# Splitting weight chunks three ahead of the one in use, in place of two

## The chip, the cores and the metric

The kernel runs on one core of a Trainium2 chip. The time is that of the device for one execution, in microseconds (us); lower is better. Names used below: TensorE (PE; its weight loads are listed as PEld), VectorE (DVE), ScalarE (ACT), GpSimd (POOL) and SyncE (SP, whose queue issues most loads).

## What is computed

Two consecutive layers of an encoder over 256 positions of 2048 channels, all in float32.

```python
h = rms_norm(x, norm_mix[layer])
if layer % 2 == 0:   # one input projection: pooling channels, queries, keys, values
    mixed = concatenate([pool_out, att_out]) @ w_out_ab[e]     # multi-scale pooling, 12-head attention (4 key heads)
else:
    mixed = mlstm_mixer(h, w_in_c[o], b_gate_c[o], h_norm_c[o], w_out_c[o])   # 8 heads, both directions
x = x + mixed
x = x + conv_ffn(rms_norm(x, norm_ffn[layer]), w_up[layer], conv_w[layer], conv_b[layer], w_down[layer])
```

`conv_ffn` is an up-projection to 2 x 5632 channels, a width-3 convolution over positions, a SiLU gate and a down-projection back to 2048.

## The kernel before

**Weights in chunks.** All the weights pass once through the core as a single list of 881 chunks, each 128 partitions by 1024 float32 (512 KB). TensorE multiplies in the float32r format, so each operand is cut in two: a high part, which is a cast, and a low part, which is the rest. A product is then high times high, high times low and low times high. For a chunk of weights this is `split` (L123): a cast on ScalarE (L134; on VectorE for the very first piece) and a subtraction on VectorE (L135), into a tile `hl` that holds both parts.

**Buffers.** Raw chunks go into the pool `wraw` (L230), which has 6 buffers; split chunks into `wsplit` (L231), which has 4. So the load of chunk k must wait for the split of k-6, and the split of chunk k for TensorE's last matmul with k-4.

**How far ahead.** The class `Stream` (L93) keeps the list. TensorE's code calls `next` (L154) for each chunk, and that calls `ahead`, which first issues what lies ahead and then hands out the chunk. `la` is how many chunks ahead loads are issued (5), `sa` how many ahead splits are issued. `st = Stream(nc, behind, wp, sp, weights, 5, 2)` at L247 sets both; in `attention_layer` `sa` is 1 during the key projection and is set again at L733.

```python
def ahead(self, i, split=None):                       # L142
    n = len(self.srcs)
    ...
    while self.n_load < min(n, i + self.la + 1):
        if self.n_load >= self.n_split + self.la - self.sa + 1:
            self.split()
        self.load()
    while self.n_split < min(n, i + (self.sa if split is None else split) + 1):
        self.split()
```

Some chunks of the down-projection are sums of two or more pieces of weights. They go through a tile `sum` (3 buffers): a load on SP (L119) and a DMA on GpSimd's queue that adds (L120), and for the chunk that follows, two adds on VectorE (L130, L131).

**Order of the work.** TensorE's order is that of the code. ScalarE, VectorE, SP and GpSimd are ordered when the program is built, by a scheduler that works from a model of the times and takes the order of the code as the priority (the key projection alone is fixed by hand on ScalarE, VectorE and SP too). Each engine then runs its list strictly in order. So the place in the code at which a split is issued sets its priority against the rest of ScalarE's and VectorE's work.

**The stages.** First the key projection (`kproj`), the first query projection (`qproj0`), values, further queries with the attention heads woven in between, the two pooling groups, and the output projection (`op`). Then the FFN of layer 0: 44 up-projections (`up`, 64 matmuls of 4 chunks each; `stat_group`, L374), and between them units of a down-projection with fewer products (Winograd's form of Strassen's scheme, `pp`, `unit` at L1035). Their products are drained from PSUM by `drain` (L1069, adds at L1081) and put together by `total` (L1091, L1098). Each up-projection is followed by a gather (L438, L439), a multiplication (L996), six convolution steps on ScalarE (L1001 to L1003), two adds on VectorE (L1004, L1005), the gate (L1009, L1010) and a split of the result (L1011, L1012); `combine` (L1014) makes the sums of operands (L1018 to L1025). The last slice of channels goes through an ordinary down-projection in four blocks of 512 columns (`dn`, `down_two` at L1148, `down` at L1132). Its tiles come from the pool `mm` of two PSUM tiles, and `residual` (L445, L448) adds each block to `x` in two halves; when both halves have been read, the tile is free for the block after next. Where a layer follows, `norm.add` squares the new block on ScalarE (L345) and transposes it on TensorE (L323). Then the second mixer (`mv`, `mq`, `mk`, `mo`, `op`) and the FFN of layer 1, which ends with the output.

Beside this run premix DMAs (L485), issued on ScalarE's and GpSimd's queues and paced by TensorE's matmuls, which add pieces of down-projection weights in DRAM ahead of their use.

Of the kernel before, what the change touches and what calls it, by code (L numbers as in the profile page):

```python
# [216 lines left out]
def trunk(ctx: ExitStack, tc: tile.TileContext, gx, xT, xn, call, catt, cml, weights, mixes, out):  # L217
# [29 lines left out]
    st = Stream(nc, behind, wp, sp, weights, 5, 2)  # L247
# [165 lines left out]
    def mov_group(act, name, width=512, before=None, after=None):  # L413

        ps = mmp.tile([P, 2, 512 if width > 256 else width], F32, tag="mm", name=name)
        per = CH * P // width
        hl = None
        for k in range(KT):
            if k % per == 0:
                before and before(k)  # L420
                hl = st.next()
                after and after(k)
            src = act(k)
            c = (k % per) * width
            terms = [(t, i, j) for t in range(2) for i, j in ((0, 0), (0, 1), (1, 0))]
            if before and k == 0:
                terms.sort(key=lambda e: e[1:])
            for t, i, j in terms:
                first, last = k == 0 and (width > 256 or t == 0), k == KT - 1 and (width > 256 or t == 1)
                mm(ps[:, t, :width], src[:, i, t * P : t * P + P], hl[:, j, c : c + width],  # L430
                   first and i + j == 0, last and i == 1)
            wv.tick(1.29 * width / 512)
        return ps
# [60 lines left out]
    def attention_layer(norm, nxt):  # L494
        with ExitStack() as es:
# [234 lines left out]
            st.split(then)  # L730
            st.sa = 1
            ps = mov_group(xx, "kproj", 512, ahead, tables)
            st.sa = 2  # L733
            first.close()
            catb.extend(actp.tile([P, 8, 2, S], F32R, tag=f"B{i}", name=f"cat{i}") for i in range(2))
            wv.add(k_block(ps))
# [452 lines left out]
    norms = [Norm(0), None]  # L1189
    norms[1] = Norm(1)  # L1190
    attention_layer(norms[0], norms[1])
    norms.append(Norm(2))
    ffn_layer(0, norms[1], norms[2])
# [265 lines left out]
```

## Time and profile before

| | us |
|---|---|
| three runs | 2162.14, 2163.13, 2166.14 |
| median | 2163.13 |
| the profiled execution's own time | 2162.39 |
| its span, from the first to the last instruction | 2160.3 |

The granted TensorE clock was 1.000 over the span. HBM was read and written at 294 GB/s over the span. Loads of 512 KB took 4.7 to 5.6 us at the median from issue to landing, and the two DMAs of a sum 5.7 and 9.6 us.

How to read the rows: a group row has line, engine, operation, tile written and tiles read, shape and count, and then busy time, mean in ns, idle time before it and what ended most of that. A row of waits has who waited for whom, the total in us, the number of times and the longest. A row of the timeline has start, length, engine, line, operation and count, and in brackets the idle time before it and what ended it. A row of the chain of waits has start, length and name: the chain is followed back from the last instruction, at each step to what released it. Ends of matmuls are modelled, so the starts are the better guide to TensorE's pace.

### The profile page before, as it was taken

How to read it: one execution, taken by the hardware profiler on the slowest of the kernel's cores; microseconds unless marked ns; L12 is line 12 of the kernel's file. 1: busy time of each engine (PE TensorE's matmuls, PEld its weight loads, DVE VectorE, ACT ScalarE, POOL GpSimd, SP SyncE). 2: the span in 40 equal slices, each digit the busy share in tenths (PEclk: the TensorE clock that was granted, in tenths of full speed). 3: DMA queues.
4: the chain of work that ended last, by engine and by line, in shares of the span. 5: the costliest groups of instructions: out<-in, count | busy, mean ns of one | idle time of the engine just before them, and what ended most of it. 6: DMA issues, size and time to landing. Idle time of an engine off the chain costs nothing.

```text
span 2160.3 us, 31974 instructions
## 1 busy us (share of the span) xinstructions
PE 2151.2 (100%) x11394; PEld 1840.4 (85%) x11394; DVE 1752.4 (81%) x2453; ACT 1421.7 (66%) x2219; POOL 225.2 (10%) x286
## 2 busy tenths in 40 slices
PE   9999999999999999999999999999999999999999
PEld 7888888888888888889888888888888888888887
DVE  7676678899889888987777676667889898988988
ACT  7665577767677767766454544457877777776774
POOL 0012111111100100001111111211100010100000
PEclk9999999999999999999999999999999999999999
DMA  9668989899989877778888887888978897987675
GB/s 327 211 202 240 294 247 312 248 314 304 297 297 290 294 258 234 265 239 249 229 253 244 242 248 227 273 272 251 289 226 290 286 290 264 280 271 253 228 252 196
DMA packets 167281, 566.24 MB, mean 262 GB/s; under 512 B 21098, under 2 KB 23698, under 8 KB 167122
## 3 DMA queue, kind: packets, MB, share of 16 engines
q1 hardware_dynamic: 130640, 467.54, 61.7%
q0 software_dynamic: 22240, 56.90, 15.7%
q10 hardware_dynamic: 14242, 39.77, 5.8%
q8 instruction: 89, 1.46, 0.3%
q14 instruction: 70, 0.57, 0.1%
HBM read 561.98 MB, written 73.44 MB: 294 GB/s over the span
## 4 chain that ended last, share of the span: by engine, by line
PE 91%; DVE 3%; DMA 3%; ACT 1%; issue 1%; ACTq 0%; DVEq 0%; POOLq 0%
PE up L272 41%; PE pp L272 14%; PE op L272 8%; PE mv L272 4%; PE mq L272 4%; PE mk L272 4%; PE mo L272 4%; PE dn L272 3%; PE qproj L272 3%; DVE hl L135 2%; DMA sum<-in_dn 1%; DMA w<-in_up 1%; PE vproj L272 1%; PE kproj L272 1%; PE av L272 1%
## 5 line engine op out<-in xcount | busy, mean ns | idle before, releaser
L135 DVE TENSOR_TENSOR hl<-w,hl 128x1024 fp32r<-128x1024 f32 (+2 forms) x843 | 1014.4, 1215 | 207.6 <-ACT hl L134 204.6
L134 ACT CAST hl<-w 128x1024 fp32r<-128x1024 f32 (+2 forms) x842 | 866.3, 1047 | 440.2 <-PE up L272 138.4
L272 PE MATMUL up<-xx,hl 128*128 128x512 f32 (+1 forms) x5632 | 994.2, 337 | 0.9 <-DVE hl L135 0.9
L272 PEld LDWEIGHTS up<-xx,hl 128*128 128x128 f32 x5632 | 866.8, 188 | 131.7 <-DVE hl L135 1.9
L272 PE MATMUL pp<-hl,s 128*128 128x512 f32 x888 | 221.8, 391 | 1.6 <-DVE hl L135 1.5
L272 PEld LDWEIGHTS pp<-hl,s 128*128 128x128 f32 x888 | 163.4, 188 | 36.3 <-DVE hl L135 4.7
L485 POOL DMA_DIRECT2D m<-m x136 | 108.4, 799 | 743.8 <-PE up L272 347.2
L272 PE MATMUL pp<-hl,g 128*128 128x512 f32 x666 | 169.5, 390 | 0.0
L272 PEld LDWEIGHTS pp<-hl,g 128*128 128x128 f32 x666 | 122.4, 188 | 23.7
L438 ACT COPY tb_up<-up 128x512 f32<-128x512 f32 x88 | 51.6, 587 | 120.6 <-PE up L272 120.6
L485 POOL DMA_DIRECT2D m<-in_dn x68 | 57.0, 838 | 601.1 <-PE up L272 271.5
L1004 DVE TENSOR_TENSOR y<-y,z 128x510 f32<-128x510 f32 x88 | 60.6, 689 | 53.5 <-ACT y L1003 53.4
L1003 ACT ACTIVATE y<-tb_up,conv 128x256 f32<-128x256 f32 x176 | 103.7, 589 | 0.0
L439 DVE TENSOR_TENSOR tb_up<-up,tb_up 128x512 f32<-128x512 f32 x88 | 60.7, 690 | 42.0 <-ACT tb_up L438 41.4
L272 PE MATMUL mk<-xx,hl 128*128 128x512 f32 (+1 forms) x512 | 92.2, 337 | 0.0
L272 PE MATMUL mq<-xx,hl 128*128 128x512 f32 (+1 forms) x512 | 92.2, 337 | 0.0
L1001 ACT ACTIVATE z<-tb_up,conv 128x256 f32<-128x256 f32 x176 | 88.4, 502 | 5.2 <-DVE tb_up L996 4.3
L272 PE MATMUL mv<-hl,xx 128*128 128x512 f32 (+2 forms) x480 | 91.7, 350 | 0.0
L272 PE MATMUL op<-hl,cat 128*128 128x512 f32 x384 | 91.5, 393 | 0.0
L272 PE MATMUL mo<-hl,xx 128*128 128x512 f32 x384 | 90.5, 391 | 0.0
L272 PE MATMUL op<-hl,mcat 128*128 128x512 f32 x384 | 89.5, 392 | 0.0
L272 PEld LDWEIGHTS mq<-xx,hl 128*128 128x128 f32 x512 | 79.3, 188 | 11.6
(233 smaller groups left out, 2171.8 us busy)
## 6 DMA issues: line engine op xcount, KB each, us to landing
w<-in_up SPq DMA_DIRECT2D x352, 512.0 KB, 5.1
w<-in_dn SPq DMA_DIRECT2D x179, 512.0 KB, 5.0
w<-in_m_in SPq DMA_DIRECT2D x124, 512.0 KB, 5.6
m<-in_dn ACTq DMA_DIRECT2D x136, 256.0 KB, 5.5
w<-m SPq DMA_DIRECT2D x68, 512.0 KB, 4.8
w<-in_a_in SPq DMA_DIRECT2D x46, 512.0 KB, 4.7
sum<-in_dn SPq DMA_DIRECT2D x40, 512.0 KB, 5.7
sum<-in_dn POOLq DMA_DIRECT2D x40, 512.0 KB, 9.6
```

Of the source, the lines that this page charges most:

```text
L134: (self.nc.vector.tensor_copy if i + c == 0 else self.nc.scalar.copy)(hl[:, 0, c : c + n], w[:, c : c + n])
L135: low = self.nc.vector.tensor_sub(hl[:, 1, c : c + n], w[:, c : c + n], hl[:, 0, c : c + n].bitcast(F32))
L272: last_mm[0] = pe.matmul(out_, lhsT, rhs, start=start, stop=stop, skip_group_check=True)
L438: a.copy(tb, ps[:, :, 1, :])
L439: v.tensor_add(tb, ps[:, :, 0, :], tb)
L485: paced(eng.dma_start(to[p : p + P // 2], src[p : p + P // 2], **kw))
L1001: a.activation(z[:, 0, j, :], u[:, j, :], AF.Copy, scale=cw(tl, 0))
L1003: a.activation(y[:, j, :], u[:, j, :], AF.Identity, scale=cw(tl, 1), bias=cw(tl, 3))
L1004: v.tensor_add(y[:, :, 1:S], y[:, :, 1:S], z[:, 0, :, 0 : S - 1])
```

## The change

```diff
             st.split(then)
             st.sa = 1
             ps = mov_group(xx, "kproj", 512, ahead, tables)
-            st.sa = 2
+            st.sa = 3
             first.close()
```

From the first query projection to the end of the kernel, the call for chunk i issues splits up to i+3 in place of i+2. Loads are still issued up to i+5, and the pools keep their 6 and 4 buffers. The number of instructions is the same.

## The prediction

> **What bounds the kernel now.** I read the page first, then the waits of TensorE (PE and PEld), of ScalarE and of the SP queue, and last the timeline at the places where TensorE stops.
>
> ```profile
> PE 2151.2 (100%) x11394; PEld 1840.4 (85%) x11394; DVE 1752.4 (81%) x2453; ACT 1421.7 (66%) x2219; POOL 225.2 (10%) x286
> ...
> PE 91%; DVE 3%; DMA 3%; ACT 1%; issue 1%; ACTq 0%; DVEq 0%; POOLq 0%
> ...
> L135 DVE TENSOR_TENSOR hl<-w,hl 128x1024 fp32r<-128x1024 f32 (+2 forms) x843 | 1014.4, 1215 | 207.6 <-ACT hl L134 204.6
> L134 ACT CAST hl<-w 128x1024 fp32r<-128x1024 f32 (+2 forms) x842 | 866.3, 1047 | 440.2 <-PE up L272 138.4
> ```
>
> TensorE is busy for 2151.2 of 2160.3 us, so whatever the splits do, at most some 9 us can be won. A split is one cast on ScalarE (1.05 us) and one subtraction on VectorE (1.22 us). The next rows say what they wait for, and what waits for them (us in total, times, longest).
>
> ```profile
> PE pp L272 <- DVE hl L135: 1.5, 3, 0.7
> PE wps L296 <- DVE pad L694: 1.2, 1, 1.2
> PE up L272 <- DVE hl L135: 0.9, 1, 0.9
> ```
>
> ```profile
> PEld pp L272 <- DVE hl L135: 4.7, 8, 1.1
> PEld up L272 <- DVE hl L135: 1.9, 3, 1.3
> ```
>
> ```profile
> ACT hl L134 <- PE up L272: 151.7, 118, 1.8
> ```
>
> ```profile
> SPq L114 <- DVE hl L135: 1332.5, 638, 7.0
> ```
>
> All that TensorE waits for late splits after the first projection is 1.5 + 0.9 = 2.4 us of idle, or 4.7 + 1.9 = 6.6 us if every wait of the weight loads is counted. Splits are seldom late. They are themselves held by TensorE: there are four buffers of split weights, so the cast of chunk k starts when TensorE has left chunk k-4, and ScalarE stands idle for that (151.7 us under the up-projection alone). The loads in turn hang on the splits that free their buffers (1332.5 us). Three ahead plus the one in use are the same four buffers. So the change cannot run a split before TensorE releases its buffer. It can only change what stands in front of it on ScalarE and VectorE.
>
> **What the change moves.** The built program of after has the same instructions as that of before, on every engine. TensorE's order is the same to the last one. About 64 of ScalarE's 2277 entries and 228 of VectorE's 2423 stand elsewhere. SP has one load (chunk 543) a few places earlier, ahead of loads of sums. GpSimd has one premix DMA ahead of one accumulating DMA. Both are moved long before their data is used, and I cost them at nothing: what hides them is the out-projection of the second mixer, and if it didn't, one load is late by one issue. Nearly every move has one form: a split goes ahead of a drain of products (L1081), a sum of partials (L1098) or a conv step (L1001 to L1005) that stood before it, and that work then comes one split later. So there are two things to price: places where a split was late, and places where the postponed work is needed at once.
>
> **The one loss.** It is at the end of the first FFN, where the down-projection's third block takes over the PSUM tile of the first, as soon as both residual adds (L448) have read it.
>
> ```profile
> 942.25 1.05 ACT L134 CAST hl<-w 128x1024 fp32r<-128x1024 f32 x1 [1.62 <-PE dn L272]
> ...
> 947.27 0.63 ACT L345 ACTIVATE sq<-x 128x512 f32<-128x512 f32 x1
> 947.80 0.19 ACT L345 ACTIVATION_READ_ACCUMULATOR sq<-x 128x1 f32 x1
> 947.90 1.04 ACT L134 CAST hl<-w 128x1024 fp32r<-128x1024 f32 x1
> ```
>
> ```profile
> 945.69 1.27 DVE L448 TENSOR_TENSOR x<-x,dn 128x512 f32<-128x512 f32 x2
> 946.88 1.28 DVE L1098 TENSOR_TENSOR x<-x,acc 128x512 f32<-128x512 f32 x2
> 948.09 1.22 DVE L135 TENSOR_TENSOR hl<-w,hl 128x1024 fp32r<-128x1024 f32 x1
> ```
>
> ```profile
> 942.73 9.01 PE L272 MATMUL dn<-hl,g 128*128 128x512 f32 x39
> 951.58 0.60 PE L323 MATMUL xt<-cst,x 128*128 128x128 f32 x4
> ```
>
> By the program the cast at 942.25 is that of chunk 391, released when TensorE left 387, and the one at 947.90 is that of 393. TensorE issues a matmul every (951.58 - 942.73)/39 = 0.227 us, 12 to a chunk, 2.72 us. So it leaves 388 at 944.93 and 389 at 947.65, and issues the first matmul of 390, which opens the third block, at 947.49. In before both L448 are over by 945.69 + 1.27 = 946.96, which is 0.53 us in time.
>
> In after, VectorE's order here is L448, split 392, two L1098, split 393, second L448. Split 393 needs the buffer of 389, so its cast cannot start before 947.69. Cast 1.05, subtraction 1.22, L448 0.68 less the 0.1 by which VectorE's instructions overlap, and twice 0.04 from one engine to another: the second L448 is over at 947.69 + 1.05 + 0.04 + 1.22 - 0.1 + 0.68 = 950.58. TensorE goes on at 950.62 in place of 947.49, which is **3.1 us** lost. It is a ring: TensorE waits for an add that is queued behind a split that waits for TensorE. Nothing covers it. Behind that L448 are queued two L1098, the second block's L448 and, on ScalarE, the squares and the casts of 394 on; TensorE needs all of these later than the stall moves them. The second FFN has the same hand-over, but there both L448 keep their place ahead of the next split, and I cost it at nothing.
>
> **The gains.** Three are at places where TensorE now stops.
>
> ```profile
> 483.21 0.68 DVE L1081 TENSOR_TENSOR x<-x,pp 128x512 f32<-128x512 f32 x1
> 483.80 0.68 DVE L130 TENSOR_TENSOR w<-w,sum 128x512 f32<-128x512 f32 x1
> 484.41 1.22 DVE L135 TENSOR_TENSOR hl<-sum,hl 128x1024 fp32r<-128x1024 f32 x1
> ```
>
> ```profile
> 547.82 0.68 DVE L1081 TENSOR_TENSOR x<-x,pp 128x512 f32<-128x512 f32 x1
> 548.42 0.68 DVE L130 TENSOR_TENSOR w<-w,sum 128x512 f32<-128x512 f32 x1
> 549.02 1.22 DVE L135 TENSOR_TENSOR hl<-sum,hl 128x1024 fp32r<-128x1024 f32 x1
> ```
>
> ```profile
> 490.72 8.59 DMA sum<-in_dn
> ...
> 555.36 10.17 DMA sum<-in_dn
> ...
> 578.70 13.19 DMA w<-in_up
> ```
>
> ```profile
> 571.17 0.73 PE L272 MATMUL pp<-hl,s 128*128 128x512 f32 x2 [0.69 <-DVE hl L135]
> ```
>
> In the chain of waits the split at 484.41 frees the buffer of a sum, whose second DMA lands at 490.72 + 8.59 = 499.3; from there the chain runs over VectorE to a late chunk near 508, one of the three waits of pp above. The split at 549.02 does the same for the stop at 571.17, through the DMA that lands at 555.36 + 10.17 = 565.5. In after, one L1081 goes from in front of each of these splits to behind it, and one costs its pitch, 548.42 - 547.82 = 0.60. That is 0.6 at each place, 1.2 in all, if the DMAs take what they took. The bounds are 0 (they land when they did) and 0.69 for the second.
>
> ```profile
> 595.04 0.59 ACT L1003 ACTIVATE y<-tb_up,conv 128x256 f32<-128x256 f32 x1
> 595.54 1.98 ACT L134 CAST hl<-w 128x1024 fp32r<-128x1024 f32 x2
> ```
>
> ```profile
> 598.27 1.90 PE L272 MATMUL up<-xx,hl 128*128 128x256 f32 x10 [0.86 <-DVE hl L135]
> ```
>
> The casts at 595.54 are of 227 and 228. In after they stand ahead of the six conv steps, and their subtractions ahead of L1004 and L1005. The cast then starts when the chunk lands, which is after 226's landing (578.70 + 13.19 = 591.9) and before 595.5. Cast and subtraction end 2.3 later, between 594.2 and 597.8, against 598.2 now. I take 0.9 of the 0.86 idle and what the next start adds; bounds 0 and 1.0.
>
> ```profile
> 2118.31 0.99 PEld L272 LDWEIGHTS pp<-hl,s 128*128 128x128 f32 x5 [0.53 <-DVE hl L135]
> ```
>
> Here split 865 goes ahead of two L1098, 1.2 us earlier, and the 0.53 wait goes; about half of it is on the path, 0.3. Against that, some splits now stand behind a postponed add and come one or two adds of 0.6 later (122 and 124 near 362 to 366, 757 and 758 near 1891). The waits above say that few splits are late at all, so I take 0.3 lost, bounds 0 and 1.2. The rest of the moves is hidden: a drain may come a split later, because an up-projection of 64 matmuls, 32 of them 512 wide (32 x 0.227 = 7.3 us at the least), stands between one product's end and the next that needs its bank. Without that cover each postponed drain would cost up to a split's 1.2 us.
>
> **Sum.** +3.1 + 0.3 - 1.2 - 0.9 - 0.3 = +1.0 us. The profiled execution took 2162.39 us (span 2160.3 and 2.1 around it), 0.74 under the median of 2163.13, so I expect 2163.4 beside it and **2164.1 us** as a median.
>
> **Rivals.**
>
> 1. *The loads under the first FFN land later* (slower). Casts and subtractions that come earlier send loads out earlier into DMA rings that are full: the three landings above took 8.6 to 13.2 us. TensorE hangs on three of them. If those queue for what others gain, the 2.1 us of gains are gone, and each further 1.6 us (as an estimate, the spread of the two sums above, 10.17 and 8.59 us) is lost three times: +1.0 + 2.1 + 4.8 = +7.9, 2171.0. It decides from 0.6 us later on, where the gains end. For it: these DMAs are the chain. Against: no load is added, and only a few go out earlier, by 0.6.
> 2. *The stall comes and the gains don't*, because the landings stay: +3.1 + 0.3 - 0.3 = +3.1, 2166.2.
> 3. *The stall costs its length and then a slower clock.* The longest idle of TensorE in this trace is 1.2 us, at the start, so a gap of 3.1 is not shown. If the clock halved for one chunk, 12 matmuls would take 2.7 us more: +3.7, 2166.8. [...]
> 4. *No stall*, because the second add gets through earlier than I work out: -2.1, 2161.0.
> 5. *The change does nothing that counts*, as four buffers bind either way: 2163.1. Against it stand the moves in VectorE's order.
>
> **Chances.** Forecast 0.50; rival 1 0.14; rival 2 0.12; rival 3 0.08; rival 4 0.12; rival 5 0.04. A change of under 0.2% (4.3 us) is about what a measurement of this kernel cannot tell from none. Slower by more: 0.12 of rival 1, 0.04 of rival 3, 0.03 each of rival 2 and the forecast, together 0.22. Faster by more: 0.06 of rival 4 (if other stops go too) and 0.02 of the forecast, 0.08. Within: 0.70. The range of 2160.5 to 2168.5 leaves out most of rival 1 and the far end of rival 4.
>
> **What would show it.** After's PE should have a new wait at about 947 us, of some 3 us, on L448's x; if it is missing, the loss is wrong. The waits on hl L135 near 508, 571 and 598 should shrink or go; if they stay and the DMA rows of the chain are longer, rival 1 or 2 is right. The granted clock between 945 and 960 decides rival 3. TensorE's stretches elsewhere should last what they last now; if they don't, I have missed a wait.

## The result

After takes **2167.85 us** (median of 16 executions, 2164.58 to 2169.40), before 2162.68 (16, 2160.68 to 2166.14). The ratio is 1.0022, with a 95% interval of 1.0014 to 1.0029: slower by 3.0 to 6.3 us, by 5.2 between the medians. The forecast was +1.0. The profiled execution of after took 2167.90 us, of which the span is 2165.6.

The page of after, the rows that answer to those of before (engines, the chain's shares, the two halves of a split):

```profile
PE 2153.6 (99%) x11394; PEld 1840.7 (85%) x11394; DVE 1753.4 (81%) x2453; ACT 1423.8 (66%) x2219; POOL 225.0 (10%) x286
...
PE 91%; DVE 5%; DMA 3%; issue 1%; ACT 1%; ACTq 0%; DVEq 0%; POOLq 0%
...
L135 DVE TENSOR_TENSOR hl<-w,hl 128x1024 fp32r<-128x1024 f32 (+2 forms) x843 | 1014.0, 1216 | 219.4 <-ACT hl L134 216.7
L134 ACT CAST hl<-w 128x1024 fp32r<-128x1024 f32 (+2 forms) x842 | 867.0, 1047 | 448.1 <-PE up L272 125.3
```

Splits and casts cost what they cost before. VectorE's share of the chain is 5% in place of 3%, but 2% are some 43 us, far more than was lost, and in tail_three (below), which loses as much as after, it is 3%: the chain only takes another way there. Two things count: TensorE's own busy time grew, by 2.4 us with the same 11394 matmuls, and it has a new wait. The waits of TensorE in after name the wait:

```profile
PE dn L272 <- DVE x L448: 3.3, 1, 3.3
PE pp L272 <- DVE hl L135: 1.3, 4, 0.6
PE wps L296 <- DVE pad L694: 1.2, 1, 1.2
PE up L272 <- DVE hl L135: 0.5, 1, 0.5
PE up L272 <- ACT hl L134: 0.4, 1, 0.4
PE dn L272 <- DVE hl L135: 0.3, 1, 0.3
```

One new wait of 3.3 us, on the residual add, tops the list. The waits on splits and casts under pp, up and dn make 1.3 + 0.5 + 0.4 + 0.3 = 2.5, as much as before's 2.4. Here is the place, in the timelines of VectorE, of ScalarE and of TensorE of after:

```profile
943.11 0.68 DVE L448 TENSOR_TENSOR x<-x,dn 128x512 f32<-128x512 f32 x1
944.67 1.23 DVE L135 TENSOR_TENSOR hl<-w,hl 128x1024 fp32r<-128x1024 f32 x1 [0.88 <-ACT hl L134]
945.82 0.68 DVE L1098 TENSOR_TENSOR x<-x,acc 128x512 f32<-128x512 f32 x1
946.42 0.68 DVE L1098 TENSOR_TENSOR acc<-acc 128x512 f32<-128x512 f32 x1
947.02 1.22 DVE L135 TENSOR_TENSOR hl<-w,hl 128x1024 fp32r<-128x1024 f32 x1
948.15 0.68 DVE L448 TENSOR_TENSOR x<-x,dn 128x512 f32<-128x512 f32 x1
```

```profile
945.77 1.05 ACT L134 CAST hl<-w 128x1024 fp32r<-128x1024 f32 x1 [0.51 <-PE dn L272]
```

```profile
948.98 5.97 PE L272 MATMUL dn<-hl,g 128*128 128x512 f32 x18 [3.30 <-DVE x L448]
954.78 0.60 PE L323 MATMUL xt<-cst,x 128*128 128x128 f32 x4
```

TensorE leaves chunk 389 at 948.98 - 3.30 = 945.68; the cast of 393 starts 0.09 later, its subtraction runs from 947.02, the second L448 behind it ends at 948.15 + 0.68 = 948.83, and TensorE goes on 0.15 later. This is the ring of the forecast. The longer busy time is in the length of TensorE's row: 18 matmuls take 5.97 us, where the same 18 take 4.33 at full clock (the row of add_first, below). The same stretch by windows (window, its length, busy time and count of PE, PEld, DVE, ACT, POOL, then the granted clock, DMA share and GB/s):

```profile
945.70:948.90 3.20, 0.00 (x0) 0.00 (x0) 3.20 (x6) 1.05 (x1) 0.00 (x0) 1.00 0.69 213
948.90:949.50 0.60, 0.52 (x2) 0.49 (x3) 0.60 (x2) 0.58 (x2) 0.00 (x0) 1.00 0.87 121
949.50:952.90 3.40, 3.40 (x10) 2.61 (x9) 3.23 (x7) 1.41 (x6) 1.13 (x2) 0.51 0.36 124
952.90:960.00 7.10, 7.10 (x38) 5.91 (x37) 4.23 (x6) 4.41 (x9) 0.00 (x0) 0.99 0.52 100
```

TensorE idles, starts at full clock, and 0.6 us later gets **half the clock for 3.4 us** (0.51 over 949.50 to 952.90). That costs 5.97 - 4.33 = 1.64 us, called 1.65 below. Stop and clock together: 3.30 + 1.65 = 4.95 us.

The start of each matmul in after's trace, less that of the same matmul in before's, gives the rest: -1.97 ahead of the tail, +3.20 behind it (954.78 - 951.58), and +5.3 at the end, by 1.26 between 1760 and 1785, 0.6 at 1891 and 0.2 from 2118 on. The step at the tail is 5.17 by starts and 4.95 by idle time and clock; the starts count more, since idle time is counted from a modelled end (0.16) and the first matmul behind the stop takes longer (some 0.1).

### The profile page after: what moved, and what is told of

It is laid out like the page before. It is cut to its first block, busy times and chain, and to the rows that moved or that the text cites. A ratio compares the mean times of both kernels' runs of the same rounds, so it can differ in the third digit from the quotient of the medians.

```text
span 2165.6 us, 31983 instructions
## 1 busy us (share of the span) xinstructions
PE 2153.6 (99%) x11394; PEld 1840.7 (85%) x11394; DVE 1753.4 (81%) x2453; ACT 1423.8 (66%) x2219; POOL 225.0 (10%) x286
## 4 chain that ended last, share of the span: by engine, by line
PE 91%; DVE 5%; DMA 3%; issue 1%; ACT 1%; ACTq 0%; DVEq 0%; POOLq 0%
PE up L272 41%; PE pp L272 14%; PE op L272 8%; PE mv L272 4%; PE mq L272 4%; PE mk L272 4%; PE mo L272 4%; PE dn L272 3%; PE qproj L272 3%; DVE hl L135 2%; DMA sum<-in_dn 1%; PE vproj L272 1%; PE kproj L272 1%; PE pool L272 1%; DMA w<-in_up 1%
```

## The experiments

Theory "ring": these 4.95 us are the whole loss. Rivals: the loss is spread over the kernel, or the slow clock has nothing to do with the stop. In five kernels below the chunk number `i` in `Stream.next` sets `sa`; the first of them, one line:

```diff
-        i = self.at
+        i, self.sa = self.at, {386: 2, 400: 3}.get(self.at, self.sa)
```

**tail_two.** After, with this line.

> After, but two ahead again for chunks 386 to 399, the end of the first FFN; there VectorE's order is that of before, entry for entry. Theory 'ring': the stop of 3.30 us at about 949 and the 1.65 us of slow clock behind it make 4.95 of the 5.2 us. So 4.95 under after, 2162.9, and 0.2 over before; the row of PE waits on L448 of 3.3 us is gone. Rival 'spread': after is slower because splits and loads stand elsewhere in the whole kernel, and TensorE makes up for the stop later. So at most 1 us under after, 2166.9 or more. Rival 'clock of its own': the clock falls near 950 for another reason. So 3.3 under after, 2164.55, with a clock of 0.5 near 950 as in after.

Measured 2162.27, ratio to before 0.9996 (0.9987 to 1.0005). The stop and the slow clock are gone; TensorE's row there has no idle at all:

```profile
941.80 9.91 PE L272 MATMUL dn<-hl,g 128*128 128x512 f32 x43
```

So the whole loss, 5.2 us, goes with the order of fourteen chunks of 881.

**tail_three.** The other way round: `sa` stays 2 at L733 and the table is `{386: 3, 400: 2}`.

> Before, but three ahead for chunks 386 to 399; there VectorE's order is that of after. Ring: in before TensorE comes to the hand-over at 947.5, the second L448 ends at 950.6, a stop of 3.1 to 3.3 us, and if the clock falls behind it as in after 1.65 more: 4.75 to 4.95 over before, 2167.5. Spread: at most 1 us over before, 2163.7. Clock of its own: 3.2 over before, 2165.9, the clock where it falls in before, which is nowhere.

Measured 2167.70, ratio 1.0022 (1.0013 to 1.0031), as much as the whole change. PE's timeline and the window of it:

```profile
949.65 5.96 PE L272 MATMUL dn<-hl,g 128*128 128x512 f32 x18 [3.30 <-DVE x L448]
```

```profile
950.00:953.00 3.00, 3.00 (x9) 2.34 (x8) 2.96 (x7) 1.62 (x5) 0.84 (x2) 0.56 0.48 146
```

The same 3.30 and the same clock, in a kernel that is before everywhere else. The two runs together rule out a loss that is spread.

**add_first.** After, and one edge of order more, which puts the subtraction of 393 behind the second L448 (`adds` collects the adds of L448).

```diff
-            self.lows = self.lows[-3:] + [low]
+            self.lows = self.lows[-3:] + [low]; i == 393 and self.behind(low, self.adds[-3])
...
-            v.tensor_add(xs, xs, ps[:, t])
+            st.adds = getattr(st, 'adds', []) + [v.tensor_add(xs, xs, ps[:, t])]
```

> After, with one more edge of order: the subtraction of chunk 393 stands behind the second L448 of the first block, which it stood ahead of. Ring: in after the L1098 ahead of both is over at 947.0, so the second L448 would end at 947.7, and TensorE, which is ready at 945.68, would stop for 2.06 us in place of 3.30: 1.24 under after. If an idle stretch of 2.06 leaves the clock at 1.0, 1.65 more go: 2.9 under after, 2164.95; if it also halves the clock, 2166.6. Rival 'other release': TensorE waits there for something other than this add (a split, a bank, a transfer), and stays at 3.3: no change, 2167.85.

Measured 2166.86, ratio 1.0013 (1.0004 to 1.0021). VectorE's rows show the new order (L448, then split 393), and TensorE's the shorter stop:

```profile
945.42 0.68 DVE L448 TENSOR_TENSOR x<-x,dn 128x512 f32<-128x512 f32 x1
946.02 1.22 DVE L135 TENSOR_TENSOR hl<-w,hl 128x1024 fp32r<-128x1024 f32 x1
```

```profile
946.25 4.33 PE L272 MATMUL dn<-hl,g 128*128 128x512 f32 x18 [2.17 <-DVE x L448]
```

The stop is 2.17, against 2.06 worked out: it follows the add's place in VectorE's queue, so nothing else holds TensorE there. In this profile the clock stayed at 1.00 and 18 matmuls took 4.33 us:

```profile
946.90:950.30 3.40, 3.40 (x17) 2.81 (x16) 3.37 (x6) 1.07 (x3) 1.12 (x2) 1.00 0.65 159
```

But the mean clock of the span was 1.000 in 4 of the 11 executions and 0.999 in 7, and the 7 took 3.1 us more (means of 2167.3 and 2164.2). That is more than the 1.65 of one slow stretch, and what the rest is stays open; in fill4, below, the same difference is 1.8.

**add_first_look.** The same kernel once more, for a second profile.

> The same kernel as add_first, for one more profile: 7 of its 11 executions had a mean clock of 0.999 and took 3.1 us more than the 4 with 1.0, and its first profile is one of the 4. If the clock falls behind a stop of the same length (2.1 to 2.2 us) in some executions, this profile shows that stop with a clock of 0.5 behind it, or 1.0 again. If the slower executions are slower because the stop itself is longer, it shows a stop near 3.3.

Its one execution took 2165.35 us, at 0.999. PE's timeline, then the windows:

```profile
948.17 5.95 PE L272 MATMUL dn<-hl,g 128*128 128x512 f32 x18 [2.16 <-DVE x L448]
```

```profile
948.10:948.70 0.60, 0.53 (x2) 0.48 (x3) 0.60 (x1) 0.59 (x2) 0.00 (x0) 1.00 0.79 282
948.70:952.10 3.40, 3.40 (x10) 2.61 (x9) 3.37 (x6) 0.14 (x2) 1.12 (x2) 0.51 0.61 178
```

A stop of the same length, and this time the clock falls, again 0.6 us after TensorE starts and again for 3.4 us. One kernel, one stop, two outcomes: 2.17 us with the clock at 1.00 behind it, 2.16 us with 0.51. What sets the two profiles apart was not shown.

**fill12, fill4, fill8.** After with N matmuls into a tile that nobody reads, ahead of the third block (N = 12, 4, 8). They add work; no output changes.

```diff
+                if last and layer == 0 and b == 2:
+                    fill = psp.tile([P, 512], F32, tag="ps", name="fill")
+                    for _ in range(12):
+                        pe.matmul(fill, gt[:, 0, 0, :P], gt[:, 0].rearrange("p a b -> p (a b)"), start=True, stop=True, skip_group_check=True)
                 ps = mmp.tile([P, 2, 512], F32, tag="mm", name=f"dn{layer}_{c}_{b}")
```

> After, with 12 matmuls of 128x512 ahead of the third block of the last down-projection, whose result nobody reads: 12 x 0.227 = 2.72 us of TensorE's stop of 3.30 are filled and some 0.6 stay idle. It adds work that the reference doesn't have and changes no output. The add that ends the stop doesn't depend on it. Theory 'idle': the clock falls because TensorE stood idle. So the stop stays in time, the clock stays at 1.0, and 1.65 go: 2166.2. Rival 'clock of its own': 2167.85, with 0.5 near 950 as before. Rival 'add': the fill lies on the path and comes on top, at most 2.7 more: 2170.6.

> After, with 4 of the matmuls of fill12 (work that the reference doesn't have, no output changed) ahead of the third block: 4 x 0.24 = 0.96 of the 3.47 us between the blocks are filled, 2.5 stay idle in one piece. If what is left of an idle stretch decides on the clock, and 2.17 leaves it at 1.0 in a part of the executions (add_first showed 1.0 over the span in 4 of 11, 0.999 in 7), then 2.5 should lower it in more: 0.999 in most of 11, median between fill12's and after's, 2166.7 to 2167.8. If any matmul within the stretch keeps the clock up: 1.0 in all, 2165.7.

> After with 8 of the fill matmuls (work that the reference doesn't have, no output changed): 8 x 0.24 = 1.92 of 3.47 filled, 1.55 idle. The share of executions with a mean clock under 1.0 so far: 15 of 16 at 3.30 us idle in one piece (after), 11 of 11 at 3.30 (tail_three), 5 of 11 at 2.39 (fill4), 8 of 12 at 2.16 (add_first and its second profile), 0 of 11 at 0.58 (fill12). If the length decides in steps, 1.55 is under it: 1.0 in all 11, median that of fill12, 2165.7. If the share falls evenly with the length: 3 to 5 of 11, median near 2166.2.

PE's timelines of fill12, of fill4 and of fill8, where the third block starts:

```profile
947.95 2.88 PE L1141 MATMUL fill<-g 128*128 128x512 f32 x12
951.42 4.33 PE L272 MATMUL dn<-hl,g 128*128 128x512 f32 x18 [0.58 <-DVE x L448]
```

```profile
952.18 4.35 PE L272 MATMUL dn<-hl,g 128*128 128x512 f32 x11 [2.39 <-DVE x L448]
```

(This view ends at 956 us, so the row holds 11 of the 18 matmuls, most of them at half the clock.)

```profile
947.18 4.34 PE L272 MATMUL dn<-hl,g 128*128 128x512 f32 x18 [1.49 <-DVE x L448]
```

In fill12 the block starts no sooner (951.42 - 947.95 = 3.47 us behind the place where it would have started without the fill and the wait; in after it is 3.46), and still the kernel is faster: 18 matmuls take 4.33 us, the clock is 1.000 in all 11 executions, and the median is 2165.74, ratio 1.0010 (1.0002 to 1.0019), 2.1 under after where 1.65 was worked out. So **the idleness itself lowers the clock**. Fill8, with 1.49 us idle, shows the same: 1.000 in all 11, and 2165.69, ratio 1.0010 (1.0002 to 1.0019). Fill4 came to 2166.78, ratio 1.0015 (1.0006 to 1.0024). The medians alone would not tell these kernels from after, as the intervals overlap; the counts of the clock do. The count can be trusted as a sign of this stop: none of the 81 executions of before in these runs, and none of the 44 of tail_two, three_till_tail, three_150_235 and three_from_400, which don't have the stop, has a mean clock under 1.000. (Two of after's 15 show 0.998 and not 0.999; no trace here has such an execution.) All the runs with this stop:

| idle in one piece, us | kernel | executions under a mean clock of 1.000 | median, us |
|---|---|---|---|
| 0.58 | fill12 | 0 of 11 | 2165.74 |
| 1.49 | fill8 | 0 of 11 | 2165.69 |
| 2.17 | add_first and its second profile | 8 of 12 | 2166.86 |
| 2.39 | fill4 | 5 of 11 | 2166.78 |
| 3.30 | after | 15 of 16 | 2167.85 |
| 3.30 | tail_three | 11 of 11 | 2167.70 |

The profiled execution of fill4 is one of the 5, and its window shows the slow stretch:

```profile
952.80:956.20 3.40, 3.40 (x10) 2.66 (x9) 3.13 (x7) 1.43 (x5) 1.13 (x2) 0.52 0.33 114
```

At 0.58 and 1.49 us the clock held in all 22 executions, at 3.30 it fell in 26 of 27, in between (2.16 to 2.39) in 13 of 23 (for fill4 "most of 11" was expected, and it was 5).

**three_till_tail, three_150_235, three_from_400.** Parts of the change without the tail: three ahead up to chunk 385 (`{386: 2}`); for chunks 150 to 235 alone, where the forecast puts the gains (`sa` 2 at L733, `{150: 3, 236: 2}`); and from 400 on (2 at L733, `{400: 3}`).

> Three ahead until chunk 385, two from 386 to the end: the first part of the change alone (attention and the first FFN up to its tail). The prediction's gains lie there: 0.6 each at 508 and 571, 0.9 at 598, against 0.3 lost. Theory 'gains': they are in every execution, so 1.8 to 2.1 under before, 2160.7. Theory 'landings': what one trace shows there moves with the landings of loads, since the trace of tail_three, which has before's program up to there, is itself 1.30 us ahead of before's at 598; so the median stays within 0.5 of before, 2162.2 to 2163.2.

> Before, but three ahead for chunks 150 to 235 alone, where the prediction puts its gains (508, 571, 598); three_till_tail came out at 0.9992 of before, interval 0.9983 to 1.0001, so 1.7 us less, not quite told from none. If the gains lie at these three places: 1.7 to 2.1 under before again, about 2161. If they lie elsewhere, or are chance: 2162.2 to 2163.2.

> Two ahead until chunk 399, three from 400 on: the last part alone (second mixer and second FFN). After's trace loses 1.8 us on before's in the second FFN (1.35 of it at 1760 to 1785). Theory 'order': an add in front of a waiting one costs that each time, so 1.8 over before, 2164.5. Theory 'landings': tail_two and add_first have the same order there and their traces don't show the loss, so within 0.5 of before, 2162.2 to 2163.2, and its own trace doesn't stop at 1760 by the same row.

| | median, us | before beside it | ratio and interval |
|---|---|---|---|
| three_till_tail | 2161.47 | 2163.22 | 0.9992 (0.9983 to 1.0001) |
| three_150_235 | 2160.33 | 2163.13 | 0.9989 (0.9980 to 0.9998) |
| three_from_400 | 2163.24 | 2163.22 | 1.0001 (0.9992 to 1.0009) |

Three_till_tail lies between what its two theories expected. Three_150_235 speaks for the gains: three ahead gains some 2 us in the first FFN (0.0011 x 2163 = 2.4), though its interval, 0.4 to 4.3 us, only just leaves out none, and tail_two, with the same splits there, lies at 0.9996. PE's timeline of three_150_235 at the three places:

```profile
507.97 0.73 PE L272 MATMUL pp<-hl,s 128*128 128x512 f32 x2 [0.63 <-DVE hl L135]
...
568.72 2.55 PE L272 MATMUL pp<-hl,s 128*128 128x512 f32 x9
...
593.72 5.62 PE L272 MATMUL up<-xx,hl 128*128 128x256 f32 x31
```

The stops at 571 and 598 are gone, the one at 508 is not. Over all traces the place at 598 is plainest: the three kernels with two ahead there stop for 0.86, 0.45 and 0.41 us (before, tail_three, three_from_400), the nine traces with three ahead don't stop. One trace alone says little of the gains: between 160 us and the tail these nine run from 3.1 us faster than before's to 1.6 slower, 1.1 faster on the mean. From 400 on the change shows no gain or loss, and after's own loss in the second FFN is one execution's landing: VectorE waits there for a load for 3.16 us, three_150_235, with before's order, loses 0.89 at the same place, and three_from_400, with after's order, runs through where after stops. PE's timelines of after and of three_from_400:

```profile
1764.39 0.74 PE L272 MATMUL pp<-hl,s 128*128 128x512 f32 x2 [0.28 <-DVE hl L135]
```

```profile
1761.52 2.20 PE L272 MATMUL pp<-hl,s 128*128 128x512 f32 x9
```

## Why the forecast was right and wrong, point by point

- **"The one loss"**, +3.1 by the ring at the first FFN's tail: right in place, cause and, nearly, in size. The forecast counts its 3.13 from the next start that would have been, while the 3.30 are counted from the modelled end of the last matmul; on the forecast's count 3.46 was measured, 0.33 more. Of that, 0.05 is the cast, which starts 0.09 and not 0.04 after TensorE leaves 389; 0.16 is the subtraction, which starts 947.02 - (945.77 + 1.05) = 0.20 after the cast and not 0.04, since an L1098 is just ahead of it; and 0.11 is the step from the add to TensorE, 0.15 and not 0.04.
- **The clock behind it** is the step that failed. The sum had nothing for it; rival 3, "the stall costs its length and then a slower clock", had it at a chance of 0.08 and 2.7 us. Its term, a clock halved for one chunk, is an assumption that no run of before shows (none of its 81 executions above has a mean clock under 1.000); the runs showed 1.65 us lost in place of 2.7: by the windows the slow clock lasts 3.4 us (0.51), and not for the 12 matmuls of a chunk. It is the largest term that the sum lacked: with it, 1.0 + 1.65 = 2.65 of the 5.2. The stated range of 2160.5 to 2168.5 holds the measured 2167.85 near its upper end, but by its width: the sum forecast a change of 1.0 where 5.2 came.
- **The gains**, -1.2 at 508 and 571, -0.9 at 598: 598 and 571 as said. At 508 the landing came earlier, but TensorE did too, so the stop kept its 0.61. Other landings slipped: after stops for 0.40 and 0.53 at 525 and 526, where before didn't. So the trace of after is 1.97 us ahead before the tail (by the starts of matmuls), but 0.9 of that it has by 160 us, where tail_three, with before's program, is 0.8 ahead as well. What remains of the gains in after's trace is about 1.
- **The small terms**: +0.3 at 362 to 366 and 1891 came as 0.1 at 362 and 0.6 at 1891 in after's trace. -0.3 near 2118 failed: the wait at 865 goes, and the next chunk waits instead (0.30 in after, 0.31 in three_from_400). After's PE row:

```profile
2124.99 1.19 PE L272 MATMUL dn<-hl,g 128*128 128x512 f32 x4 [0.30 <-DVE hl L135]
```

- **The second FFN's hand-over at no cost**: right; the wait on L448 occurs once in after.
- **Rival 1** (landings slip and cost three times): slips there were, of 0.4 to 1 us and in changing places, but three_till_tail and three_150_235 are no slower than before, so they don't decide the time. **Rival 2** (the stall without the gains) is borne out in part: the stops at 571 and 598 go, the one at 508 stays. Rivals 4 and 5 fell with the wait of 3.3.

The parts, each against before in its own runs: +5.0 (tail_three), -1.7 (three_till_tail), 0.0 (three_from_400), together +3.3. After measured +5.2, interval 3.0 to 6.3. With intervals of 2 us to each side of each part this is no contradiction, but whether after lacks 1 to 2 us of the gains in the median, as its one trace suggests, stays open.

## The version to keep

Three_150_235 is the fastest of the kernels measured: 2160.33 us, 0.9989 of before (0.9980 to 0.9998) and some 7 us under after. Its lead over before is small, and it is the best of several, so it may be less than it looks; its interval lies wholly below that of after (1.0014 to 1.0029). Three ahead pays where splits stood behind drains that nobody was waiting for, and must stop before the tail, where an add that TensorE waits for stands in the same queue.

## What to carry to other kernels

When work is issued further ahead into a queue that runs in order, look for the instruction that it overtakes and for whoever waits for that: here a split that waits for TensorE overtook the add that TensorE waits for, and one such ring in 2160 us outweighed all the gains. Here, more lookahead without more buffers only changed the order. Count a stop of TensorE like those here (2.16 to 3.30 us) at its length plus the slow clock that may follow it (here in 39 of 50 executions, some 1.65 us), and when one trace shows gains of a microsecond from landings, test the part alone before believing them.

## What the runs showed of the hardware

In the four profiles that show it (after, tail_three, add_first_look, fill4) the granted clock of TensorE fell to half for some 3.4 us after a stop of 2.16 to 3.30 us, in one piece and beginning 0.6 to 0.8 us after TensorE had started again. After's windows place it: a clock of 1.00 over 948.98 to 949.56, of 0.50 over 949.56 to 952.97 (3.41 us), and of 1.00 again over 952.98 to 2160.

By the mean clocks it fell in none of 22 executions after 0.58 or 1.49 us of idleness, in 13 of 23 after 2.16 to 2.39, and in 26 of 27 after 3.30. The length of the stop is not all that decides: of two profiles of one kernel, add_first with 2.17 us of idleness kept its clock at 1.00, and add_first_look with 2.16 us fell to 0.51 over 3.40 us. What decides between them was not shown.
